# Turning the queries and keys of two attentions before or after they are split into high and low parts

## The chip, the cores and the metric

The kernel runs on one core of a Trainium2 chip. The metric is the device time in microseconds of one execution of the whole program; the time of a version is the median of its runs.

## The reference, cut to what matters

Two layers of a generator's backbone are computed for 512 latent tokens and 256 context tokens of width 1024. Each layer projects the normalised tokens with one matrix `w_in` and feeds four token mixers: a state-space scan, a long convolution, a windowed attention (branch `c` of the kernel) and a dense attention (branch `d`). Their results go through `w_out`, and a squared-ReLU MLP follows. The change lies in the two attentions, in how queries and keys are brought into the form in which the score products take them.

```python
def split_qkv(p):                       # 4 query heads, 2 key and value heads, 64 wide
    q = p[..., :256].reshape(b, n, 4, 64)
    k = p[..., 256:384].reshape(b, n, 2, 64)
    v = p[..., 384:].reshape(b, n, 2, 64)

yw = window_attention(apply_rope(qw, cos, sin), apply_rope(kw, cos, sin), vw, kwc, vwc, attn_sink)
yd = dense_attention(apply_rope(rms_norm(qd, q_norm), cos, sin),
                     apply_rope(rms_norm(kd, k_norm), cos, sin), vd, kdc, vdc)
# the first layer alone also runs both attentions for the context queries
s = jnp.einsum('bqgrd,bkgd->bgrqk', q_blk, k_all) * hd ** -0.5
```

Two query heads (`r`) share one key head: a "group", `kv` in the kernel.

## The kernel before, in words

Tokens lie on partitions, in six tiles of 128: tiles 0 to 3 are latent, 4 and 5 are context. All products use operands in two parts: a high part of 12 bits (type F32R) and the low part that is left. The helper `hi` (L261) writes a high part by a copy on ScalarE, and `lo` (L267, its instruction at L268) subtracts it from the source on VectorE. Weights are split by the same helpers when they are loaded (L354 and L355), so L263 and L268 appear in the rows with many tiles; the tile's name tells them apart.

A layer first runs the two attentions, `d` and then `c` (L1387 to L1392). For each of them:

- `qkv_in` (L1094) projects the tokens. Its results stand in PSUM tiles `pg` (two banks) and are copied by ScalarE to `qk` (L1111, L1113), a tile of 256 query columns and 128 key columns for each token tile.
- `qk_prep` (L1127) normalises (branch `d` alone) and rotates `qk` in place on VectorE, one token tile after the other; L1171 is the last step for a latent tile.
- `qk_split` (L1173) is called once for each of the two groups. For each pair of token tiles it makes tiles `sqk` of 128 x 128: for queries, the high and the low part of each of the two heads, for keys, the high part twice and the low part twice. There are four buffers of `sqk`. Each block of 128 columns is then turned by TensorE (L1204), four blocks to a bank `pm` of PSUM, and the two halves of a bank are copied to the operands `QK` by ScalarE (L1206) and VectorE (L1207). The result is, for each head of queries, a tile whose partitions 0 to 63 hold the high part and 64 to 127 the low part, and for the group's key two tiles, one with the high part in both halves and one with the low part.
- `attend` (L1217) is called for each group, in layer 0 also for the context queries. Scores are two products with these operands (L1247, L1248) into `ps`; then a maximum (L1254), an exponential (L1261) and a normalisation (L1267) give `P`. `P` is turned through `pm` banks (L1284), split to `pt` (`hi` and `lo`) and multiplied with the values into `po` (L1292). At the end of a head the halves of `po` are added (L1295, L1296, both on 64 partitions), which is called the merge below.

Then follow the input projections of the convolution and of the state-space branch (`hyena_in`, `ssd_in`), whose products use the same two `pg` banks. In layer 1 the context tiles have keys but no queries (`need` is false).

The order of the instructions on each engine is not written by hand: a scheduler goes through the program in the order written, with its own estimate of times, and lets work of later calls fill an engine that has nothing to do. So the projection for branch `c` and `hyena_in` run between the steps of branch `d`, and `hyena_in` and `ssd_in` between those of branch `c`. Once ordered, each engine takes its queue in that order: what stands behind a waiting instruction waits too. Banks and buffers are rings: three banks `pm`, two `pg`, one `ps` (two banks wide), one `po`, four `sqk`, eight `QK`.

Of the kernel before, what the change touches and what calls it, by code (L numbers as in the profile page):

```python
# [12 lines left out]
F32 = mybir.dt.float32  # L13
F32R = mybir.dt.float32r
BF16 = mybir.dt.bfloat16
I32 = mybir.dt.int32
AF = mybir.ActivationFunctionType
# [24 lines left out]
# columns of the packed per-partition parameters  # L42
# [3 lines left out]
# columns of the packed row parameters  # L46
# [78 lines left out]
def layout(inp):  # L125
    """The inputs as the program takes them: copies in other orders, nothing computed."""
# [52 lines left out]
def cut(x, c0, n):  # L179
    """token columns c0 .. c0 + n of a (latent, context) pair of tiles"""  # L180
    return x[0][:, c0:c0 + n] if c0 < SEQ else x[1][:, c0 - SEQ:c0 - SEQ + n]


class K:
# [16 lines left out]
    def weave(self, *gens):  # L201
        """emit several streams, each given as (generator, steps per turn)"""
# [26 lines left out]
    def push(self, name, tags, side="left", psum=False):  # L229
        """A phase's pool, tags {tag: (words, dtype, bufs)}; each side is a stack."""  # L230
# [39 lines left out]
    def rsqrt(self, ms, n, w=0):  # L270
        """ms [128, n] -> ms ** -0.5 in a new small tile (Newton from the exponent trick)."""
# [55 lines left out]
    def mlp_order(self):  # L327
        """the units of the two products, an eighth of the hidden features at a time: the second
        product of an eighth comes while the first one of the next is under way."""
# [38 lines left out]
    def tform(self, w, c0, XT, block, m=128):  # L368
        """psum[feat 128, tok] = W chunk^T x; a block of tokens (start, length)."""
# [13 lines left out]
    def nform2(self, ws, X, t, out):  # L383
        """out [tokens of tile t, 512] from four chunks of features."""
# [52 lines left out]
    def mod_section(self, l, s):  # L437
        """silu(c), silu(c_ctx) times columns 1024 s .. of w_mod: two [2, 512] rows."""
# [20 lines left out]
    def mod_sums(self, l, s, hf):  # L459
        """silu(c), silu(c_ctx) times 512 columns of w_mod on the vector engine, 128 partial sums of each."""  # L460
# [18 lines left out]
    def mod_rows(self, acc):  # L479
        """the two sums over the partitions, a row [1, 512] each"""  # L480
# [10 lines left out]
    def mod_cols(self, l, s, idx, gain=None):  # L491
        """shift (or gain * (1 + scale)) with features on partitions: [128, 8, 2]."""
# [65 lines left out]
    def pre_norm(self, xs, xrs):  # L558
        """xr = x * rsqrt(mean(x^2)) for a few tiles at once"""
# [9 lines left out]
    # eight chunks of features by tokens, two parts each: tiles of half the chunks lie together  # L569
# [1062 lines left out]
```

## Time and profile before

| | |
|---|---|
| median of 3 runs | 1932.01 us (1931.42 to 1938.32) |
| span of the profiled execution | 1931.3 us |
| instructions | 27370 |
| TensorE busy, products (PE) and weight loads (PEld) | 1803.7 us and 1480.3 us |
| VectorE (DVE) busy | 1298.2 us |
| ScalarE (ACT) busy | 836.4 us |
| mean granted clock of TensorE | 0.976 |

The profile is of one execution. Products on PE are pipelined, so that the duration of one reaches under the next one, and PE counts as busy in short gaps; on DVE and ACT, too, an instruction can begin a little before the one ahead of it ends. A granted clock of 1.00 is 2.4 GHz and 0.50 is 1.2 GHz. A row of a wait says which instruction waited, which one released it, how long in all, how often, and the longest one.

### The profile page before, as it was taken

The page shows a single profiled execution, that of the slowest core. Times are in us where ns is not written, and L with a number is a line of the kernel's source. Part 1 is how long each engine was busy: PE and PEld are TensorE (multiplying, and loading weights), DVE is VectorE, ACT ScalarE, POOL GpSimd, SP SyncE. Part 2 cuts the span into 40 slices and gives each one's busy share as a digit, 9 for nine tenths or more (in the row PEclk, how much of TensorE's full clock was granted, in tenths as well). Part 3 has the DMA queues.
Part 4 walks back from the last instruction along what each step waited for, and adds up shares of the span by engine and source line. Part 5 has one row for each costly group of instructions (what it writes and reads, how often), then busy time and mean ns, then how long its engine had stood idle before and what let it go on. Part 6 is the DMA issues. An engine that isn't in the chain of part 4 may idle for free.

```text
span 1931.3 us, 27370 instructions
## 1 busy us (share of the span) xinstructions
PE 1803.7 (93%) x10170; PEld 1480.3 (77%) x10170; DVE 1298.2 (67%) x2897; ACT 836.4 (43%) x1804; POOL 91.3 (5%) x176
## 2 busy tenths in 40 slices
PE   6899999979879999999999998899977889999998
PEld 2588888845667888888888888888866688888886
DVE  4877888877656656666666658987878563444446
ACT  3844565536515532322222327556546263232322
POOL 0120001011000000000000000000020000000000
PEclk9999999989989999999999999999989899999999
DMA  7631121278833344333333415122193243233232
GB/s 258 206 118 55 40 72 58 69 255 282 285 99 131 99 131 131 120 112 108 121 120 120 143 46 173 45 56 80 45 297 94 93 143 109 87 99 98 87 101 85
DMA packets 137597, 235.16 MB, mean 122 GB/s; under 512 B 12466, under 2 KB 77395, under 8 KB 137464
## 3 DMA queue, kind: packets, MB, share of 16 engines
q1 hardware_dynamic: 122920, 186.12, 30.2%
q0 software_dynamic: 14544, 47.30, 7.1%
q8 instruction: 80, 1.31, 0.3%
q14 instruction: 53, 0.43, 0.1%
HBM read 206.74 MB, written 26.64 MB: 121 GB/s over the span
## 4 chain that ended last, share of the span: by engine, by line
PE 62%; DVE 7%; ACT 3%; DMA 1%; issue 1%; DVEq 0%; ACTq 0%; SPq 0%
PE pg L296 17%; PE pg L297 16%; PE pg L298 16%; PE py L296 2%; PE py L297 2%; PE py L298 2%; PE po L1292 1%; PE pm L1284 1%; PE ps L1247 1%; PE psd L1050 1%; PE pn L591 0%; PE pm L1204 0%; PE ps L1248 0%; DVE w L268 0%; PE ph L296 0%
## 5 line engine op out<-in xcount | busy, mean ns | idle before, releaser
L263 ACT ACTIVATE w<-r 128x1024 fp32r<-128x1024 f32 (+1 forms) x176 | 186.5, 1061 | 351.2 <-PE pg L298 348.6
L268 DVE TENSOR_TENSOR w<-r,w 128x1024 fp32r<-128x1024 f32 (+1 forms) x176 | 214.3, 1223 | 109.5 <-ACT w L263 108.5
L296 PE MATMUL pg<-xl,w 128*128 128x512 f32 (+1 forms) x704 | 273.0, 391 | 2.5 <-DVE ya L1309 1.4
L298 PE MATMUL pg<-xl,w 128*128 128x512 f32 (+1 forms) x704 | 273.7, 390 | 0.0
L297 PE MATMUL pg<-xl,w 128*128 128x512 f32 (+1 forms) x704 | 272.8, 388 | 0.0
L296 PE MATMUL pg<-w,H 128*128 128x512 f32 x640 | 250.1, 391 | 0.0
L297 PE MATMUL pg<-w,H 128*128 128x512 f32 x640 | 249.3, 390 | 0.0
L298 PE MATMUL pg<-w,H 128*128 128x512 f32 x640 | 249.0, 389 | 0.0
L474 DVE SCALAR_TENSOR_TENSOR x<-r,scT,x 128x512 f32<-128x512 f32 x168 | 119.1, 746 | 70.9 <-DMA r<-in_w_mod_dram 70.9
L296 PEld LDWEIGHTS pg<-xl,w 128*128 128x128 f32 x704 | 132.8, 190 | 30.2 <-issue 2.2
L298 PEld LDWEIGHTS pg<-xl,w 128*128 128x128 f32 x704 | 133.6, 190 | 26.1
L297 PEld LDWEIGHTS pg<-xl,w 128*128 128x128 f32 x704 | 133.8, 190 | 25.6 <-DVE xl L268 0.2
L296 PEld LDWEIGHTS pg<-w,H 128*128 128x128 f32 x640 | 120.1, 188 | 26.9 <-issue 1.8
L1518 ACT ACTIVATE t<-pg 128x512 f32<-128x512 f32 (+1 forms) x100 | 50.4, 506 | 205.7 <-PE pg L298 195.5
L298 PEld LDWEIGHTS pg<-w,H 128*128 128x128 f32 x640 | 120.1, 188 | 24.9
L297 PEld LDWEIGHTS pg<-w,H 128*128 128x128 f32 x640 | 120.1, 188 | 24.7
L1549 DVE TENSOR_TENSOR ya<-pg,ya 128x512 f32<-128x512 f32 x120 | 82.0, 687 | 69.8 <-PE pg L298 69.5
L1520 DVE TENSOR_TENSOR t<-t 128x512 f32<-128x512 f32 (+1 forms) x100 | 58.1, 582 | 89.9 <-ACT H L1519 89.7
L296 PE MATMUL pg<-xc,w 128*128 128x256 f32 (+1 forms) x368 | 103.4, 284 | 1.1 <-ACT xc L263 1.1
L298 PE MATMUL pg<-xc,w 128*128 128x256 f32 (+1 forms) x368 | 104.0, 283 | 0.0
L297 PE MATMUL pg<-xc,w 128*128 128x256 f32 (+1 forms) x368 | 103.9, 283 | 0.0
L296 PE MATMUL pg<-w,xl 128*128 128x256 f32 (+1 forms) x320 | 92.3, 290 | 5.6 <-ACT qk L1111 2.6
(357 smaller groups left out, 3859.2 us busy)
## 6 DMA issues: line engine op xcount, KB each, us to landing
r<-in_mlp_w_dram SPq DMA_DIRECT2D x128, 512.0 KB
r<-in_w_mod_dram SPq DMA_DIRECT2D x80, 512.0 KB
r<-in_w_in_dram SPq DMA_DIRECT2D x40, 512.0 KB
ht<-in_inv_dram POOLq DMA_DIRECT2D x20, 512.0 KB, 5.4
ht<-in_fwd_dram POOLq DMA_DIRECT2D x18, 512.0 KB, 5.3
wm<-in_w_mod_dram SPq DMA_DIRECT2D x16, 512.0 KB
r<-in_w_out_dram SPq DMA_DIRECT2D x16, 512.0 KB
xd<-x POOLq DMA_DIRECT2D x16, 512.0 KB, 3.3
```

What stands on the lines that cost most here:

```text
L263: self.nc.scalar.activation(dst, src, AF.Copy)
L268: self.nc.vector.tensor_tensor(dst, src, h.bitcast(F32), SUB)
L296: mm(out, ah, bh, start=first, stop=False)
L297: mm(out, ah, bl, start=False, stop=False)
L298: mm(out, al, bh, start=False, stop=last)
L474: nc.vector.scalar_tensor_tensor(acc[:, c], raw[:, k], sc, acc[:, c], MUL, ADD)
L1050: nc.tensor.matmul(py[:, 64 * hh:64 * hh + 64], Ms[d][:, hh // 2, hh % 2, :], xdt[:, d, hh, :], start=d == 0, stop=d == 1)
L1247: nc.tensor.matmul(ps[:, o:o + kn], qs, KS[0][:, k0:k0 + kn], start=True, stop=False)
L1284: nc.tensor.transpose(p[:, n:n + 128], P[:, col:col + 128], self.ident)
L1518: nc.scalar.activation(r, p[:, :nn], AF.Relu)
L1520: nc.vector.tensor_tensor(r, r, r, MUL)
L1549: nc.vector.tensor_tensor(dst, p, dst, ADD)
```

## The change

`qk_split` is now called once for both groups. It turns the raw `qk` tiles, 128 columns at a time: the two key heads together, and the two query heads of a group together. The blocks of four latent tiles (or of the two context tiles) go side by side into one `pm` bank. The split is made out of PSUM: ScalarE copies the rows of one head, 64 partitions, to the high part of the operand, and VectorE subtracts that high part from the same rows of PSUM and writes the low part. For a key, both are done twice, once for each half of the partitions. The keys come before the queries. The tiles `sqk` are gone. (The diff also drops comments and docstrings; they are left out here.)

```diff
-    def qk_split(self, l, kv, qk):
+    def qk_split(self, l, qk):
...
-        QS = [self.a("QK") for _ in range(2)]
-        KS = [self.a("QK") for _ in range(2)]
-        for pair in range(3):
-            SQ, SK = [], []
-            for t in (2 * pair, 2 * pair + 1):
-                src = qk[t // 2][:, t % 2]
-                if t < 4 or need:
-                    sq = self.a("sqk", (2, 2, 64))
-                    q_ = src[:, 128 * kv:128 * kv + 128].rearrange("p (h d) -> p h d", d=64)
-                    self.hi(sq[:, :, 0], q_)
-                    self.lo(sq[:, :, 1], q_, sq[:, :, 0])
-                    SQ.append(sq)
-                sk = self.a("sqk", (2, 2, 64))
-                kk = src[:, 256 + 64 * kv:320 + 64 * kv].unsqueeze(1).to_broadcast([128, 2, 64])
-                self.hi(sk[:, 0], kk)
-                self.lo(sk[:, 1], kk, sk[:, 0])
-                SK.append(sk)
-            cs = slice(256 * pair, 256 * pair + 256)
-            jobs = []
-            if SQ:
-                jobs += [([q[:, hh] for q in SQ], QS[hh]) for hh in range(2)]
-            jobs += [([k_[:, hl] for k_ in SK], KS[hl]) for hl in range(2)]
-            for j in range(0, len(jobs), 2):
+        QS = [[self.a("QK") for _ in range(2)] for _ in range(2)]
+        KS = [[self.a("QK") for _ in range(2)] for _ in range(2)]
+        lo, hi = slice(0, 64), slice(64, 128)
+        for t0, cnt in ((0, 4), (4, 2)):
+            n = 128 * cnt
+            cs = slice(128 * t0, 128 * t0 + n)
+            src = [qk[t // 2][:, t % 2] for t in range(t0, t0 + cnt)]
+
+            def turned(c0):
                 p = self.a("pm")
-                for jj in range(2):
-                    for i in range(2):
-                        nc.tensor.transpose(p[:, 256 * jj + 128 * i:256 * jj + 128 * i + 128],
-                                            jobs[j + jj][0][i].bitcast(F32).rearrange("p a d -> p (a d)"), self.ident)
-                nc.scalar.activation(jobs[j][1][:, cs], p[:, 0:256], AF.Copy)
-                nc.vector.tensor_copy(jobs[j + 1][1][:, cs], p[:, 256:512])
-        return QS, KS
+                for i in range(cnt):
+                    nc.tensor.transpose(p[:, 128 * i:128 * i + 128], src[i][:, c0:c0 + 128], self.ident)
+                return p
+
+            p = turned(256)
+            for kv in range(2):
+                r = slice(64 * kv, 64 * kv + 64)
+                H, L = KS[kv]
+                for d in (lo, hi):
+                    nc.scalar.activation(H[d, cs], p[r, :n], AF.Copy)
+                for d in (lo, hi):
+                    nc.vector.tensor_tensor(L[d, cs], p[r, :n], H[r, cs].bitcast(F32), SUB)
+            if t0 == 0 or need:
+                for kv in range(2):
+                    p = turned(128 * kv)
+                    for hh in range(2):
+                        r = slice(64 * hh, 64 * hh + 64)
+                        Q = QS[kv][hh]
+                        nc.scalar.activation(Q[lo, cs], p[r, :n], AF.Copy)
+                        nc.vector.tensor_tensor(Q[hi, cs], p[r, :n], Q[lo, cs].bitcast(F32), SUB)
+        return list(zip(QS, KS))
 
     def attention(self, l, br, qk, V):
-        ops = [self.qk_split(l, kv, qk) for kv in range(2)]
+        ops = self.qk_split(l, qk)
...
         ra = self.push("attR", {"P": (768, F32, 4), "tA": (512, F32, 1), "tP": (384, F32, 2), "yt": (512, F32, 1),
-                                "QK": (768, F32R, 8), "pt": (1024, F32R, 2), "sqk": (256, F32R, 4)}, "right")
+                                "QK": (768, F32R, 8), "pt": (1024, F32R, 2)}, "right")
```

## Rows read from the trace of the kernel before

**Rows 1.** The page, part 1: busy us, share, instructions.

```profile
PE 1803.7 (93%) x10170; PEld 1480.3 (77%) x10170; DVE 1298.2 (67%) x2897; ACT 836.4 (43%) x1804; POOL 91.3 (5%) x176
```

**Rows 2.** The page, part 4: chain that ended last, by engine.

```profile
PE 62%; DVE 7%; ACT 3%; DMA 1%; issue 1%; DVEq 0%; ACTq 0%; SPq 0%
```

**Rows 3.** Stretches of 20 us, layer 0: busy us (instructions), clock, DMA share, GB/s.

```profile
160.00:180.00 20.00, 17.61 (x133) 17.13 (x133) 17.53 (x55) 5.73 (x21) 0.00 (x0) 0.91 0.09 28
180.00:200.00 20.00, 18.68 (x145) 17.05 (x144) 17.34 (x45) 12.93 (x41) 0.00 (x0) 1.00 0.19 54
200.00:220.00 20.00, 19.82 (x154) 18.48 (x153) 18.58 (x48) 11.81 (x30) 0.00 (x0) 1.00 0.00 1
...
280.00:300.00 20.00, 19.76 (x131) 16.80 (x130) 18.68 (x57) 15.49 (x48) 2.16 (x4) 1.00 0.30 93
```

**Rows 4.** The same of layer 1 (PE, PEld, DVE, ACT, POOL as above).

```profile
1220.00:1240.00 20.00, 15.53 (x112) 14.31 (x111) 17.99 (x52) 10.67 (x36) 0.00 (x0) 0.91 0.18 53
...
1320.00:1340.00 20.00, 19.99 (x114) 16.15 (x113) 16.43 (x45) 13.51 (x35) 1.15 (x2) 1.00 0.33 104
```

**Rows 5.** Groups by form, the old split: busy us, mean ns, idle before, releasers.

```profile
L1204 PE MATMUL pm<-ident,sqk 128*128 128x128 f32 x176 | 31.9, 288 | 5.2 <-DVE sqk L268 4.9
L263 ACT ACTIVATE sqk<-qk 128x128 fp32r<-128x128 f32 x88 | 24.3, 306 | 26.8 <-PE pm L1204 14.4 <-DVE qk L1171 10.7 <-ACT qk L1111 0.9
L268 DVE TENSOR_TENSOR sqk<-qk,sqk 128x128 fp32r<-128x128 f32 x88 | 22.3, 284 | 3.6 <-ACT sqk L263 3.4
L1207 DVE CAST QK<-pm 128x256 fp32r<-128x256 f32 x44 | 17.9, 419 | 1.9 <-ACT QK L1206 1.4
L1206 ACT ACTIVATE QK<-pm 128x256 fp32r<-128x256 f32 x44 | 15.9, 376 | 3.7 <-PE pm L1204 3.6
```

**Rows 6.** Timeline of PE in layer 0: start, us, engine, line, count.

```profile
190.33 1.03 PE L1204 MATMUL pm<-ident,sqk 128*128 128x128 f32 x8
191.20 0.27 PE L1284 MATMUL pm<-ident,P 128*128 128x128 f32 x1
```

**Rows 7.** Groups by form: copies and sums out of PSUM.

```profile
L1295 ACT ACTIVATE tA<-po 64x512 f32<-64x512 f32 x16 | 9.5, 593 | 14.3 <-PE po L1292 14.2
L1295 ACT ACTIVATE tA<-po 64x256 f32<-64x256 f32 x8 | 3.0, 380 | 4.1 <-PE po L1292 4.0
L1296 DVE TENSOR_TENSOR yt<-po,tA 64x512 f32<-64x512 f32 x16 | 10.9, 684 | 1.0 <-ACT tA L1295 0.4
L1296 DVE TENSOR_TENSOR yt<-po,tA 64x256 f32<-64x256 f32 x8 | 3.3, 417 | 0.9 <-ACT tA L1295 0.8
L268 DVE TENSOR_TENSOR pt<-pm,pt 128x512 fp32r<-128x512 f32 x80 | 53.0, 687 | 11.6 <-ACT pt L263 10.9
```

**Rows 8.** Timeline of DVE in layer 0, d split and c split.

```profile
189.66 0.89 DVE L268 TENSOR_TENSOR sqk<-qk,sqk 128x128 fp32r<-128x128 f32 x4
...
281.89 0.42 DVE L1296 TENSOR_TENSOR yt<-po,tA 64x256 f32<-64x256 f32 x1
282.33 0.15 DVE L1259 TENSOR_SCALAR s<-s 128x1 f32<-128x1 f32 x1
282.40 0.41 DVE L1207 CAST QK<-pm 128x256 fp32r<-128x256 f32 x1
```

**Rows 9.** Instructions of tile QK, whole program: who waited for it.

```profile
  PEld pm L1204: 0.5, 2
```

**Rows 10.** Waits of PE, whole program: us in total, times, longest.

```profile
PE pm L1204 <- DVE sqk L268: 4.9, 3, 2.4
PE pg L296 <- ACT qk L1111: 2.6, 1, 2.6
```

**Rows 11.** Stretches of 2 us behind the two d splits' stalls.

```profile
176.00:178.00 2.00, 2.00 (x12) 2.00 (x11) 0.57 (x3) 0.30 (x3) 0.00 (x0) 0.50 0.04 8
...
1230.00:1232.00 2.00, 2.00 (x12) 2.00 (x10) 1.61 (x7) 1.76 (x5) 0.00 (x0) 0.50 0.37 77
```

**Rows 12.** Timeline of DVE ahead of layer 0's first transpose.

```profile
171.91 0.55 DVE L1171 TENSOR_TENSOR qk<-qk,tP 128x384 f32<-128x384 f32 x1
...
173.05 0.28 DVE L268 TENSOR_TENSOR sqk<-qk,sqk 128x128 fp32r<-128x128 f32 x1
```

## The prediction

> **What bounds the kernel now.** I read the busy times of the page first: TensorE (PE) is busy for 93% of the span, VectorE (DVE) for 67%, ScalarE (ACT) for 43% [rows 1]. Then the chain of work that ended last: 62% of it lies on PE, and what is not PE is DVE first, 7% [rows 2]. So a time saved on PE is worth most; a time saved on ACT alone is worth nothing in itself. But the change touches only the two attentions of each layer, so the table by stretches of 20 us decides. In layer 0's attention stage PE is busy 19.82 and 19.76 us of 20 in an undisturbed stretch and in the split of branch c, and 17.61 and 18.68 us around the split of branch d [rows 3]; layer 1 looks alike, with 15.53 us around its d split [rows 4]. DVE is close behind in all of them: 17.3 to 18.7 us [rows 3], 16.4 to 18.0 us [rows 4]. Two things are to be seen: PE is the bound, with DVE near enough to take its place, and the two d splits are the two places where PE stands still.
>
> What the split costs now is in the groups by form: 176 transposes, 88 high parts on ACT, 88 low parts on DVE and 44 + 44 copies out of PSUM [rows 5]. The count follows the code: in layer 0 a branch turns 48 tiles into 12 banks, in layer 1, which has no context queries, 40 into 10, and there are two branches each: 2 x (48 + 40) = 176.
>
> **The change part by part.**
>
> *Transposes.* Now a tile of raw queries holds both heads of a group and a tile of raw keys both groups, and no low part is turned. Layer 0: 6 key tiles and 2 x 6 query tiles, 18 for a branch; layer 1: 6 + 2 x 4 = 14. In all 2 x (18 + 14) = 64, so 112 go. Eight in a row took 1.03 us, and a transpose by itself 0.27 us, so each takes (1.03 - 0.27) / 7 = 0.109 us of PE's time [rows 6]: 112 x 0.109 = 12.2 us. The upper bound is the busy time of the group, 31.9 us, by its count: 112/176 x 31.9 = 20.3 us [rows 5]; that counts the latency of each as if nothing ran under it, so I take 12.2. Not all of it shortens the stage: weight loads fill 18.48 of 20 us in one full stretch and 16.80 in another [rows 3], 88% on average, and in the rest PE waits in gaps too short to show. I take 88% of 12.2: **-10.7 us**. This lies on the path because PE has other products at hand in that stage (the next projections), which move up.
>
> *ACT.* Removed: 24.3 + 15.9 = 40.2 us busy [rows 5]. Added: per branch 8 copies of 512 columns and, in layer 0, 8 of 256, in layer 1 only 4; in all 32 and 24, each on 64 partitions. The nearest rows have this shape: 593 ns and 380 ns [rows 7]. 32 x 0.593 + 24 x 0.380 = 28.1 us. ACT is freed of 12 us; the sum counts nothing, because PE covers it.
>
> *DVE.* Removed: 22.3 + 17.9 = 40.2 us [rows 5]. Added: as many subtractions as ACT has copies, PSUM less SBUF on 64 partitions: 684 and 417 ns in the nearest rows [rows 7]; a subtraction over 128 partitions takes 687 ns [rows 7], so half the lanes save nothing. 32 x 0.684 + 24 x 0.417 = 31.9 us. Busy time falls by 8.3 us. Now how far these overlap. Four low parts in a row take 0.89 us at 0.283 each, 0.203 us from start to start [rows 8], so what is removed took 88 x 0.203 + 17.9 = 35.8 us of the engine. A 64-partition sum of the merge starts at 281.89 and takes 0.42, and the next instruction starts at 282.33, behind its end; the one after that starts at 282.40, under the 0.15 us of the one before it [rows 8]. Priced by that row all 56 new ones stand end to end, and DVE is freed of 35.8 - 31.9 = 3.9 us only. The Trainium skill, VectorE: DVE Perf Modes, section Two Vector instructions with no wait between them, says that an instruction whose output starts in another quadrant of partitions than the last one waits until all earlier ones are finished; the new code writes partitions 0 and 64 by turns, so the rule speaks against it, and the row agrees. The forecast's sum doesn't change by it, since it counts nothing for DVE, but it gives the second rival its price.
>
> *PSUM banks.* The bank of a transposed row is read by ACT and DVE in turn. Before, a bank had one copy each: 44 x (0.376 + 0.419) = 35.0 us of holding [rows 5]. After, the keys' latent bank has four and four, 4 x (0.593 + 0.684) = 5.1 us, their context bank 4 x 0.797 = 3.2 us, a query bank two and two, 2.55 or 1.6 us [rows 7]. With 4, 4, 8 and 4 of them: 20.4 + 12.8 + 20.4 + 6.4 = 60.0 us. The extra 25 us, over three banks of the ring, cost PE from 0 to 8.3 us. PE waited 0.5 us in all for a bank to be copied out so far [rows 9], which is next to the lower end: **+1.0 us**.
>
> *The stalls of the d splits.* The first transpose of a split stands in PE's queue until the low part of its tile is there: 4.9 us in three waits [rows 10]; PE waited another 2.6 us for the projection's copy [rows 10] that stood on ACT behind high parts, which waited 10.7 us for the rotation and 14.4 us for a slot of the buffer that the change drops [rows 5]. Behind each of the two stalls the granted clock is 0.50, its lower level of 1.2 GHz, for at least one stretch of 2 us [rows 11], 1.0 us lost each. Upper bound of the gain: 4.9 + 2.6 + 2 x 1.0 = 9.5 us. What will be late next is the rotation itself: the raw transposes wait for it, and in layer 0 the last latent tile's ends at 171.91 + 0.55 = 172.46 us, while the low part that released PE began at 173.05 and ended at 173.33 [rows 12]. That is 0.9 us earlier, and about the same for layer 1: **-1.8 us**. That the row of keys needs four tiles and not two costs nothing here, as the first low part stood behind the fourth tile's rotation anyway [rows 12].
>
> *Waits that are added.* A key row writes the tiles of both groups at once, and the second group's tiles are still read by the scores of the attention before. On ACT stand the projections' and the probabilities' copies behind such a write. I cost it at nothing, because attention d is almost over when the first copy of the c split starts now, at 282.40: its next-to-last head is merged at 281.89 [rows 8], and a head's scores come well before its merge. Without that cover it would be the rest of one context head. No DMA is moved, and neither SP's nor POOL's queue gets another order of its own; the buffer that goes frees space that nobody waits for.
>
> *Sum.* 1931.3 (profiled span) - 10.7 + 1.0 - 1.8 = 1919.8. The median of the runs is 1932.0, 0.7 above the span, so the forecast is **1920.5 us**.
>
> **The rivals.**
>
> *The stalls go as well.* ACT is no longer held by the dropped buffer, copies the projection out in time, and PE runs through the rotation at the full clock: 12.2 + 9.5 = 21.7 us less, 1910.3. For it: the ACT waits of the group [rows 5]. Against: DVE is busy 17.5 us of 20 there [rows 3], and the rotation still must end first.
>
> *DVE takes the place of PE.* The stage then shrinks by what DVE is freed of, 3.9 us: 1928.1. For it: 18.68 of 20 us in the c split, 17.99 in layer 1's d split [rows 3, 4], and the next instruction behind the 64-partition one's end [rows 8]. By the Trainium skill's rule cited above this would be the price of every new subtraction. Against: PE is fuller than DVE in all four stretches of layer 0 [rows 3], and DVE's share of the chain is 7% [rows 2].
>
> *The banks bind: slower.* PE takes its queue in order. If a transpose of the probabilities or the next row stands behind a key bank that is held 5.1 us in place of 0.8, PE stops for 4.3 us and loses another 1.0 us at the lower clock, as behind the stalls of now [rows 11]. In each of the four branches that is 21.2 us, less 10.7: 1942.5. It decides from 10.7 / 4 = 2.7 us a branch on. Against: the 0.5 us of now [rows 9].
>
> *The change does what it says*, but the order of all instructions is worked out anew from the program, and work moves between gaps at no gain: this lies within the second rival's time.
>
> **How the numbers follow.** Forecast 0.50 (own range 1915 to 1925), the stalls go 0.15, DVE binds or no gain 0.27, banks bind 0.08. What a measurement of this kernel can tell from no change is 0.5%, 9.7 us; the bound of faster is 1922.3. Faster: 0.15 and 0.40 of the forecast's 0.50, together 0.55. Within: the other 0.10, 0.27, and 0.02 of the banks: 0.39. Slower: 0.06. The range for 8 in 10 leaves out the banks and the far end of the stalls: 1910 to 1931.
>
> **What would show it.** Right: 64 transposes, PE's busy time down by 12 to 20 us, PE as full in the c splits as now, the wait of the first transpose now put down to the rotation. DVE the bound: its busy share near 20 of 20 us in the stage and PE's below 19. Banks: PE waiting for the new copies out of PSUM by whole microseconds, and more stretches at 0.50. Wrong would make it above all a saving on PE that turns into short gaps, which the 88% only estimates.

## The result, and the profile after

The changed kernel is slower: 1950.83 us in the median (1948.91 to 1956.57), against 1933.24 for the kernel before beside it; the ratio is 1.0092, 95% interval [1.0072, 1.0112]. That is 17.6 us more where the prediction had 11.5 less, and outside its range. The profile is of the slowest of the four executions (1956.57, a span of 1954.8 us), so that against the profiled kernel before (1931.3) it shows 23.5 us of loss and not 17.6.

The page of the changed kernel, part 1 (busy us, share, instructions) and the first line of part 4 (the chain that ended last, by engine):

```profile
PE 1803.2 (92%) x10058; PEld 1484.2 (76%) x10058; DVE 1294.2 (66%) x2821; ACT 832.0 (43%) x1728; POOL 91.9 (5%) x176
...
PE 67%; issue 17%; DVE 8%; DMA 4%; ACT 3%; POOL 2%; SPq 0%; POOLq 0%; DVEq 0%; ACTq 0%
```

Against [rows 1, 2]: 112 matmul records fewer, as the change says, and yet PE is busy as long as before. The mean granted clock is 0.961 instead of 0.976, and at the lower clock a product takes longer: in this trace products of one form (`ph<-hx,ht`) start 0.21 us apart at 420.2 to 423.0 us, where the granted clock is 0.50, and 0.12 us apart at 429.0 to 431.0, where it is 1.00. The chain has a new second entry, "issue", 17%; in the runs below this share does not follow the time (9% in e17, 1% in the slower e18), so nothing is read from it.

The split's groups by form (busy us, mean ns, idle time before, its releasers):

```profile
L1190 PE MATMUL pm<-ident,qk 128*128 128x128 f32 x64 | 11.7, 293 | 8.2 <-DVE qk L1171 6.8 <-DVE QK L1200 1.4
L1209 DVE TENSOR_TENSOR QK<-pm,QK 64x512 fp32r<-64x512 f32 x16 | 11.0, 690 | 1.1 <-ACT QK L1208 0.6
L1200 DVE TENSOR_TENSOR QK<-pm,QK 64x512 fp32r<-64x512 f32 x16 | 11.0, 689 | 7.0 <-ACT QK L1198 6.9
L1198 ACT ACTIVATE QK<-pm 64x512 fp32r<-64x512 f32 x16 | 9.5, 593 | 4.0 <-DVE QK L1200 2.2 <-PE pm L1190 1.5
```

They are what [rows 5] became: 64 transposes, and copies and subtractions at the durations read off [rows 7]. What the change says of its own work it does. So the loss lies elsewhere.

Stretches of 20 us of the changed kernel (us, then busy us and instructions of PE, PEld, DVE, ACT, POOL; granted clock, DMA share, GB/s):

```profile
160.00:180.00 20.00, 17.51 (x140) 16.68 (x140) 18.14 (x36) 9.52 (x19) 0.00 (x0) 1.00 0.09 28
180.00:200.00 20.00, 17.58 (x136) 16.23 (x133) 18.07 (x47) 9.51 (x28) 0.00 (x0) 1.00 0.10 27
...
280.00:300.00 20.00, 19.41 (x128) 17.14 (x128) 17.75 (x35) 13.71 (x28) 2.22 (x4) 1.00 0.12 37
380.00:400.00 20.00, 13.20 (x58) 10.51 (x58) 15.84 (x44) 10.47 (x28) 2.17 (x4) 0.64 0.28 93
400.00:420.00 20.00, 11.60 (x64) 5.41 (x64) 7.24 (x23) 2.70 (x6) 2.15 (x4) 0.50 0.70 222
```

and two of the same stretches of the kernel before:

```profile
380.00:400.00 20.00, 19.30 (x125) 16.36 (x123) 17.36 (x53) 12.44 (x33) 3.24 (x6) 1.00 0.30 102
400.00:420.00 20.00, 10.76 (x59) 4.94 (x63) 14.32 (x28) 6.69 (x14) 2.74 (x5) 0.66 0.92 301
```

Around the two splits the stretches answer to [rows 3] without anything striking. The difference is at 380 to 420 us, where the attention of layer 0 ends. Before, PE is full up to the end (125 instructions) and DVE has 14.32 us of work while the next stage's loads come in. Now 58 instructions are left for PE, its clock is at 0.50, the lower level of 1.2 GHz, and DVE has 7.24 us.

What is missing there lies earlier. Counted in PE's queue, as the traces have it, the products of the next projections that stand ahead of the score tiles of branch c are: before, 19 ahead of the first tile, then 32, 18, 5, 7, and 14, 9, 25, 21, 24, 6 ahead of the last six, some 44 more after that. Now 46, then 38, 47, 10, 13, and 22, 12, 25, 0, 0, 0 ahead of the last six, none after. The program is the same there; its order is not.

The order of issues has changed too. Waits of SP's queue, 370 to 440 us, and its timeline, changed kernel:

```profile
SPq L445 <- PE pg L447: 23.9, 5, 20.6
```

```profile
382.98 23.96 SPq L445 DMA_DIRECT2D r<-in_w_mod_dram  x4
406.99 1.05 SPq L772 DMA_DIRECT2D hz<-us  x2
```

and the timeline of SP's queue before:

```profile
396.36 0.82 SPq L772 DMA_DIRECT2D hz<-us  x2
```

The next stage begins with the loads of `hz`. They were issued 2.0 us ahead of the attention's last merge (398.4 us); now SP stands at a load of the modulation's weights for 20.6 us, and they come 1.3 us behind it (405.7).

By stages, with the exact borders (first sums of branch d's norm to the last merge of branch c, and on to the end of `w_out`; the same for layer 1, and on to its first `w_out` result), before:

```profile
158.97:398.38 239.41, 234.07 (x1578) 206.19 (x1577) 204.27 (x551) 136.31 (x357) 16.41 (x30) 0.99 0.19 60
398.38:618.34 219.96, 185.69 (x1125) 132.99 (x1124) 142.92 (x357) 102.89 (x267) 17.07 (x32) 0.91 0.67 223
1211.63:1405.77 194.14, 185.08 (x1205) 158.68 (x1205) 166.42 (x435) 109.83 (x277) 8.28 (x15) 0.99 0.20 62
1405.77:1523.86 118.09, 89.82 (x494) 71.25 (x493) 88.43 (x189) 54.72 (x150) 11.77 (x22) 0.87 0.54 179
```

and after:

```profile
155.02:405.65 250.63, 235.36 (x1541) 205.56 (x1543) 211.02 (x525) 139.02 (x326) 18.08 (x33) 0.96 0.20 63
405.65:637.86 232.21, 188.98 (x1107) 137.86 (x1096) 134.92 (x344) 98.37 (x258) 15.45 (x29) 0.86 0.61 205
1232.28:1444.55 212.27, 194.16 (x1205) 166.71 (x1204) 177.32 (x416) 115.10 (x254) 11.38 (x20) 0.96 0.24 76
1444.55:1547.56 103.01, 78.57 (x440) 61.94 (x441) 74.68 (x171) 46.78 (x138) 9.04 (x17) 0.87 0.50 165
```

Layer 0 loses 11.2 us in the attention and 12.2 us behind it; layer 1 loses 18.1 in the attention and wins 15.1 behind it, 3.0 us in all. So most of the loss lies in layer 0. (The border at which its attention begins comes 4.0 us earlier in the changed kernel, so that its end comes only 7.3 us later.) The attentions lose time although 60 and 52 transposes have gone from them, and DVE is busy 7 and 11 us longer in them although its split got cheaper: work of the projections has moved in.

### The profile page after: what moved, and what is told of

It is laid out like the page before. It is cut to its first block, busy times and chain, and to the rows that moved or that the text cites. A ratio compares the mean times of both kernels' runs of the same rounds, so it can differ in the third digit from the quotient of the medians.

```text
span 1954.8 us, 26976 instructions
## 1 busy us (share of the span) xinstructions
PE 1803.2 (92%) x10058; PEld 1484.2 (76%) x10058; DVE 1294.2 (66%) x2821; ACT 832.0 (43%) x1728; POOL 91.9 (5%) x176
## 4 chain that ended last, share of the span: by engine, by line
PE 67%; issue 17%; DVE 8%; DMA 4%; ACT 3%; POOL 2%; SPq 0%; POOLq 0%; DVEq 0%; ACTq 0%
PE pg L296 17%; PE pg L297 17%; PE pg L298 17%; PE py L296 2%; PE py L297 2%; PE py L298 2%; PE po L1294 2%; DMA ht<-in_inv_dram 1%; PE pm L1286 1%; PE ps L1249 1%; PE pf L675 1%; PE ps L1250 1%; PE psd L1050 1%; DVE w L268 1%; DMA hf<-spec 0%
```

## The experiments

No kernel below leaves work out. Times are medians, with the ratio to the kernel before on the same chip.

| kernel | split | order | us | ratio, 95% interval |
|---|---|---|---|---|
| changed | new | planned anew | 1950.83 | 1.0092 [1.0072, 1.0112] |
| e1_group | new, by groups | planned anew | 1958.46 | 1.0142 [1.0117, 1.0167] |
| e2_engine | new, copies first | planned anew | 1955.40 | 1.0127 [1.0096, 1.0158] |
| e3_pair | new, 2 tiles a bank | planned anew | 1960.99 | 1.0147 [1.0123, 1.0172] |
| e4_pad | new, 4 KB taken | as changed | 1954.12 | 1.0118 [1.0090, 1.0146] |
| e5_gate | new | 48 products moved back | 1962.07 | 1.0137 [1.0088, 1.0186] |
| e6_double | old, transposes twice | planned anew | 1968.62 | 1.0170 [1.0119, 1.0222] |
| e7_keys | keys new | planned anew | 1949.21 | 1.0074 [1.0051, 1.0097] |
| e8_queries | queries new | planned anew | 1953.94 | 1.0089 [1.0061, 1.0117] |
| e9 | new, modulation moved | attentions as changed | 1966.35 | 1.0164 [1.0147, 1.0181] |
| e10 | old, modulation moved | attentions as before | 1955.96 | 1.0107 [1.0085, 1.0128] |
| e11 | new, modulation earlier | planned anew | 1955.82 | 1.0113 [1.0089, 1.0137] |
| e12_reordered | old, one more buffer | planned anew | 1951.32 | 1.0089 [1.0071, 1.0107] |
| e13 | new | as before | 1943.16 | 1.0047 [1.0029, 1.0065] |
| e14 | old | as changed | 1963.48 | 1.0141 [1.0119, 1.0164] |
| e15 | new | issues alone as before | 1976.97 | 1.0215 [1.0196, 1.0234] |
| e16 | new, by groups | as before | 1948.26 | 1.0071 [1.0050, 1.0092] |
| e17 | queries new | as before | 1944.07 | 1.0066 [1.0044, 1.0088] |
| e18 | new, 2 tiles a bank | as before | 1954.97 | 1.0119 [1.0098, 1.0141] |

### First theory: the products run out before the attention ends

Four kernels change how the new split is laid out. The theory was that the long split of branch c lets the planner pull the projections' products ahead, so that none are left for the attention's end. The rivals were banks of PSUM held too long, and the changed places in SBUF.

```diff
 e1_group: the first group's operands first, the key bank turned once for each group
-            p = turned(256)
-            for kv in range(2):
...
+        for kv in range(2):
+            for t0, cnt, n, cs, src in ranges:
+                key(turned(256, src, cnt), kv, n, cs)
+                query(kv, t0, cnt, n, cs, src)
 e2_engine: all copies of a bank, then all its subtractions
 e3_pair
-        for t0, cnt in ((0, 4), (4, 2)):
+        for t0, cnt in ((0, 2), (2, 2), (4, 2)):
...
-            if t0 == 0 or need:
+            if t0 < 4 or need:
 e4_pad (once a layer; the buffer's tag is back as well)
...
+            for _ in range(4):
+                nc.vector.memset(self.a("sqk")[:, 0:1].bitcast(F32), 0.0)
```

> The new split with the first group's operands brought out first: the key bank is turned once for each group (82 transposes in place of 64, 18 more at 0.11 us = 2 us of PE), the copies and subtractions are the same 56 and 56. Theory (the split's chain up to the first scores has grown, projections were put into it, and none is left beside the last tiles of branch c, so PE stands nearly bare at the lower clock there and behind it): in PE's queue 8 to 20 products now stand ahead of each of the last tiles of branch c where the changed kernel has 0, so the time goes back to 1920 to 1935 us. Rival A (64-partition copies and subtractions are what costs): nothing of them changes, 1948 to 1953 us. Rival B (the freed space moved the buffers of the next stage onto others): unchanged too, 1948 to 1953 us.

> All copies of a bank on ScalarE first, then all its subtractions on VectorE; the same instructions otherwise. In PE's queue layer 0 is as in the changed kernel (0 products ahead of the last three tiles of branch c), layer 1 has 12 to 29 ahead of each of its last tiles again where the changed kernel has 0. Theory: layer 0's loss of some 24 us stays, layer 1's of some 4 us goes: 1944 to 1949 us. Rival A (the turns of the two engines at a bank, and 64-partition work, are the cost): both layers gain alike, 1935 to 1943 us. Rival B (buffers' places): 1948 to 1953 us.

> Two tiles to a bank in place of a row of four, so more and shorter copies and subtractions (80 of each, all of 256 columns, in place of 32 of 512 and 24 of 256: on VectorE 80 x 0.417 = 33.4 us for 31.9). PE's queue has 0 products ahead of the last three tiles of branch c in layer 0, and 12 to 31 in layer 1. Theory: as the engine-by-engine run, 1944 to 1950 us. Rival A (a bank held long is the cost): short holds bring it back in both layers, 1925 to 1938 us. Rival B: 1948 to 1953 us.

> The changed kernel with the 4 KB of the dropped buffer still taken, so that every later buffer lies where it lay before; the order on PE is the changed kernel's. Theory and rival A: no change against the changed kernel, 1948 to 1953 us. Rival B (the places of the next stage's buffers decide which loads wait for the attention's end): back to 1920 to 1935 us.

Measured: 1958.46, 1955.40, 1960.99 and 1954.12 us. The bank rival fell with e3 and the place rival with e4. But the theory fell as it was put, with e1: its queue keeps 11, 20, 15, 8, 14 and 15 products for the last six tiles, as the kernel before does, and it is no faster. In all four the attention of layer 0 takes 250.6 to 252.5 us.

Then the products were held back directly, and the two halves of the change were made alone. In e5 the last quarter of the state-space input takes its banks from the attention's own rings, so it can't start before the last tiles have left them.

```diff
 e5_gate
-                    p = self.tform(w, 128 * c, XT, (o0, nn))
+                    bank = ("ps", "pm")[i % 2] if q == 1 and c == 1 else "pg"
+                    p = self.tform(w, 128 * c, XT, (o0, nn), bank=bank)
 e6_double (kernel before)
-                    for i in range(2):
+                    for i in (0, 0, 1, 1):
 e7_keys, e8_queries: the new split for one of the two, the old one for the other
```

> The changed kernel, with the last products of the state-space input (the last quarter of its x projection, in both layers) put into a score bank and an evacuation bank of the attention instead of the projections' own, so that they can't begin before the attention's last tiles have left these banks. In layer 0 this puts 48 products behind the start of the last score tile, where the kernel before has some 44 and the changed one none. Theory (the fillers run out before the attention ends, and their work on DVE lies inside it): the attention of layer 0 ends 4 to 8 us sooner than in the changed kernel, TensorE's stretch at 0.50 behind it is under 25 us instead of 37.5, and the time is 1938 to 1947. Rival (the new split itself, its chain of ACT and DVE, is what makes the attention longer, wherever the fillers lie): the attention still takes 250 us, the time stays at 1949 to 1956. A third outcome, slower than 1956, would say that the attention's tail wants the products that were taken from it.

> The kernel before, with each of the split's 176 transposes made twice into the same place, so that only TensorE has more to do: 176 x 0.109 us = 19.2 us at full clock. If TensorE's sum sets the time, as the prediction had it for 88% of such work, the time is some 1932 + 17 = 1949. If in the attention something other than TensorE's sum sets the end (the theory now: the chain of the attention over DVE), it is 1930 to 1941.

> One part of the change alone: keys are turned raw, four tiles to a bank, and split on the way out; queries keep the split ahead of the transposes. The order that comes out keeps products for all of the attention's last tiles (23, 27, 19, 14, 13, 15 ahead of the last six in layer 0). Theory (what costs is that no products are left for the end of the attention): 1922 to 1936. Rival (the key bank, held by four copies and four subtractions of 64 partitions one behind the other, is what makes the split slow): 1943 to 1955, about the changed kernel's own.

> The other part alone: queries are turned raw and split on the way out, keys keep the split ahead of the transposes. The order that comes out keeps products for the attention's last tiles too (16, 10, 12, 7, 22, 7 in layer 0). Theory (products left for the end): 1922 to 1938. Rival (the copies and subtractions of 64 partitions cost, in queries as in keys; queries have the smaller number of them to a bank): 1936 to 1946.

Two stretches of e5:

```profile
380.00:400.00 20.00, 15.21 (x56) 12.02 (x57) 9.51 (x42) 7.53 (x23) 1.08 (x2) 0.57 0.12 39
400.00:420.00 20.00, 12.06 (x69) 8.54 (x68) 14.06 (x26) 6.82 (x13) 3.27 (x6) 0.74 0.80 265
```

The work behind the end is back (DVE 14.06 us, 14.32 before), but the attention is only 2.8 us shorter (247.9 us), its tail is still bare, at 0.57, and the stage behind it takes 238.8 us: what was held back is not what stood at the front. e5 is no faster than the changed kernel; its time is in the third outcome (over 1956), though the intervals of the two ratios overlap. In e6 the attention of layer 0 takes 240.9 us, 1.5 more than before with 96 x 0.109 = 10.5 us more for PE, and layer 1's 11.0 more; in layer 0 the projections gave way: ScalarE's last step for them (L912) ends 22.9 us behind the attention instead of 14.0, and the stage behind it is 26.9 us longer. So it answers neither column: 1968.62, twice what the sum of PE gives. e7 and e8 have nearly all of the loss with half of the edit, although products are left at the end. A cost that is about the same for each half and for the whole points to something that the three share, and an order planned anew is such a thing.

### Second theory: transfers bind the stage behind the attention

The DMA share right behind the end of layer 0's attention is 0.92 [the stretch at 400 above], and 32.8 MB moved at 298 GB/s over the 110 us from 398 to 508. Half of that (16.3 MB) are the modulation's weights.

```diff
 e9 (changed kernel), e10 (kernel before)
-ME = (4, 1, 2)
+ME = (4, 0, 3)
 e11 (changed kernel)
+        early = 1 if l == 0 else 0
+        self.do(*self.mod_list(l)[:early])
         self.ssd_in(l, XT)
...
```

> The changed kernel with one of the four modulation sections (eight loads of 512 KB, 4.2 MB) taken from the stage behind layer 0's attention and put among the products of layer 0's MLP, where the transfers' share is 0.38; the order of both attentions stays the same. Theory (in layer 0 the time is the end of the attention plus a stage behind it that is bound by its 33 MB of transfers, 298 GB/s in the kernel before): the stage behind the attention, 118.9 us, shortens by 8 to 15 us (4.2 MB at 273 to 298 GB/s are 14 to 15 us), and the time is 1936 to 1944. Rival (that stage is set by TensorE and its clock, 41 us of it at 0.50): it shortens by no more than the section's 32 small products, 4 us, and the time is 1946 to 1953.

> The same edit on the kernel before, with the order of its attentions unchanged. Theory (transfers bind the stage behind the attention, at a share of 0.91 there): its 110.1 us shorten by 8 to 15 us, and the time is 1918 to 1926. Rival (TensorE): 1929 to 1936.

> The changed kernel with one modulation section of layer 0 (4.2 MB, 32 small products) moved ahead into the attention of layer 0, where the transfers' share is about 0.2; it gets a bank of PSUM of its own there, the attention's evacuation banks are two instead of three. Theory (transfers bind the stage behind the attention): that stage shortens by 8 to 15 us, the attention lengthens by the products (some 4 us) and by what the missing bank costs, 0 to 8: 1936 to 1952. Rival (TensorE binds both stages): the products only move, the bank costs: 1951 to 1960.

Measured: 1966.35, 1955.96 and 1955.82 us. In e9 the stage from the attention's end to the end of `w_out` shortens by 9.3 us (232.2 to 222.9), though up to the state's last sums, the border that the expectation had, by 0.9 only; in e10 it lengthens by 3.1 (220.0 to 223.1), 6.4 up to the nearer border, with 4.2 MB less to move. In the two the MLP takes 17 and 27 us more, and that is most of what they lose. In e11 the stage shortens by 8.8 us (to 223.4), but the attention, with two `pm` banks and the added products, takes 10.9 us more (261.5), and the time is the rival's. So bytes alone don't set that stage, and moving them won nothing; the theory fell. What e9 and e10 do show: with an attention order unchanged, the attention's length repeats, 251.7 against 250.6 us and 238.7 against 239.4, and layer 1's 211.7 against 212.3 and 192.5 against 194.1.

### Third theory: the order

```diff
 e12_reordered (kernel before)
-"sqk": (256, F32R, 4)}, "right")
+"sqk": (256, F32R, 5)}, "right")
```

> The kernel before with a fifth buffer for the split parts, and nothing else: the split, its transposes and its copies are the same, but another order is planned for all engines (15, 29, 13, 16, 11, 2 products ahead of layer 0's last six score tiles instead of 14, 9, 25, 21, 24, 6). If the new split itself lengthens the attention (its 250 us against 239), this one stays near the kernel before: attention of layer 0 at 238 to 243 us, time 1929 to 1937. If any new order of this work loses what the order of the kernel before has, whatever the split: attention 246 to 253 us, time 1942 to 1956.

1951.32 us: one more buffer, nothing in the split or elsewhere rewritten, and the loss is that of the changed kernel. Its stages:

```profile
153.89:396.47 242.58, 235.99 (x1585) 207.62 (x1584) 205.16 (x552) 137.64 (x358) 16.32 (x30) 0.99 0.18 58
396.47:634.03 237.56, 190.18 (x1118) 136.04 (x1117) 142.90 (x357) 102.93 (x267) 17.05 (x32) 0.87 0.62 207
1227.13:1428.45 201.32, 193.15 (x1257) 167.31 (x1256) 174.19 (x451) 114.67 (x287) 10.27 (x18) 0.99 0.21 65
```

It loses in other places: 3.2 us in the attention of layer 0, 17.6 behind it, 7.2 in the attention of layer 1, of which 3.8 come back behind that. And it has 46 products behind the last score tile of layer 0, as the kernel before has 44, and yet its stage behind the attention is the longer one by 17.6 us: where the products lie is not by itself what costs. So my expectation mixed two things: the attention stayed near the kernel before, as the first column has it, and the time is the second column's.

Then the two were separated. In e13 and e14 all instructions outside the split stand in a given order on each engine; only the split's own find their places between them. In the traces these instructions do stand, on all five engines, in the order asked for, and the edges add none: 26976 instructions in e13 as in the changed kernel, 27371 in e14 against 27370 before. e15 gives such an order to the issues on SP and POOL alone.

```diff
 e13: the changed kernel in the order of the kernel before; e14: the other way round
+        own = [x for i, x in enumerate(L) if i not in free and str(x.engine) == "EngineType." + e ...]
+        for a, b in zip(o[:-1], o[1:]):
+            k.tc.add_manual_dep(own[int(b)], own[int(a)].name, info, reason="order")
...
 e15
+    pin(k, ("SP", "Pool"))
```

> The changed kernel, its new split as it is, but every other instruction of all five engines (PE, DVE, ACT, and the issues on SP and POOL) kept in the order that the kernel before has, by edges of order alone, without semaphores; only the split's own instructions find their places between them. If the new order is what costs, and the split itself is worth what the prediction had for it, the time is 1916 to 1928. If the order costs and the split is worth nothing, 1929 to 1936. Rival (the new split itself lengthens the attention, whatever the order): 1942 to 1953.

> The opposite pair: the old split, and every other instruction in the order that the changed kernel has. If the order costs and the split's gain is real: 1951 to 1968 (the changed kernel's time and up to 10 us more for its 112 transposes). Rival (the new split itself costs): 1928 to 1940.

> The changed kernel with the DMA issues alone, those on SP and on POOL, in the order of the kernel before; TensorE, DVE and ACT planned anew, ahead of layer 0's attention tiles as in the changed kernel. If the stage behind the attention is slow because its loads are issued in another order (12 of the 23 us that layer 0 has lost), that stage is back at 220 to 225 us and the time is 1936 to 1943. If the order of the engines' work is what costs, 1946 to 1955.

| | order of before | order of the changed kernel |
|---|---|---|
| old split | 1 (before) | 1.0141 [1.0119, 1.0164] |
| new split | 1.0047 [1.0029, 1.0065] | 1.0092 [1.0072, 1.0112] |

e14's time is in its first column (1951 to 1968). e13's 1943.16 misses the first two and lies in its rival's range (1942 to 1953).

Read down the right column: at the changed kernel's order the new split is worth 1.0092 - 1.0141 = -0.49%, 9.5 us, give or take 5.8 by the two intervals. Read along the upper row: with the old split that order costs 1.41%, 27.3 us. This is one way from the kernel before to the changed one. The other way goes by e13: down the left column the same split costs 0.47%, 9.1 us, and along the lower row the same order costs 0.45%, 8.7 us, give or take 5.2. Each way adds up to the result, so neither share can be named without saying which step comes first.

In e13 and e14 a split stands in an order that was planned for the other one. If this misfit costs as much in the one as in the other, it is (0.47 + 1.41 - 0.92) / 2 = 0.48%; then the order by itself costs 0.93%, 18 us, and the split is worth nothing. e12, in which nothing is crossed, lost 17. That the two misfits are equal is an assumption and not shown. Shown is that the new order costs time with either split, and that what the split is worth changes its sign with the order.

Stages of e14:

```profile
157.79:415.14 257.35, 242.60 (x1601) 212.14 (x1603) 212.50 (x565) 141.64 (x366) 18.01 (x33) 0.96 0.19 61
415.14:642.00 226.86, 183.60 (x1107) 132.59 (x1096) 134.72 (x344) 98.24 (x258) 15.43 (x29) 0.89 0.62 210
1236.02:1451.33 215.31, 200.88 (x1257) 173.29 (x1256) 178.88 (x452) 118.00 (x290) 11.37 (x20) 0.95 0.24 75
```

The old split in this order makes the attentions 6.7 and 3.0 us longer than the changed kernel has them, for 60 and 52 transposes, and the stage behind layer 0's 5.3 us shorter. With the same split as the kernel before they are 17.9 and 21.2 us longer than there: that is the order's doing, the old split's misfit in it included. Behind layer 1's attention 15.1 us come back (118.1 to 103.0 up to the first result of `w_out`), as in the changed kernel: of the 102 products that the kernel before has behind the last score tile there, these two have none left. Stages of e13, its longest wait of PE, and what stands there on PE's timeline:

```profile
158.31:400.98 242.67, 229.03 (x1518) 201.23 (x1517) 203.92 (x511) 134.07 (x317) 16.22 (x30) 0.99 0.18 59
400.98:628.61 227.63, 189.18 (x1125) 136.40 (x1124) 142.93 (x358) 102.93 (x267) 17.11 (x32) 0.89 0.65 215
1221.85:1423.56 201.71, 183.87 (x1153) 158.12 (x1153) 166.00 (x399) 107.54 (x241) 8.22 (x15) 0.96 0.19 59
```

```profile
PE pm L1190 <- DVE QK L1200: 13.9, 5, 4.8
```

```profile
282.76 0.40 PE L296 MATMUL pg<-xl,w 128*128 128x512 f32 x1
286.98 0.83 PE L1190 MATMUL pm<-ident,qk 128*128 128x128 f32 x4 [3.82 <-DVE QK L1200]
```

In the old order PE is busy 5.0 us less in the attention of layer 0 (60 transposes at 0.109 us are 6.5), and idle 8.3 us more (13.6 instead of 5.3): a row of raw transposes stands at a bank that the keys' subtractions still read, with nothing but its own queue behind it. The stage behind it, where neither the order nor the work differs, takes 227.6 us against 220.0, so nothing under 8 us there is read as an effect of an edit. The changed kernel waits for the keys' banks 1.4 us in all. So the planner's new order avoids the wait; that it moved the products for this reason is argued, not shown.

e15 lies outside both columns: with the issues on SP and POOL as before, it is the slowest of all. Its engines were planned anew around these issues and are near the changed kernel's order, not in it (554 of PE's 10058 matmul records stand elsewhere in its queue). Two waits of SP's queue between 370 and 420 us:

```profile
SPq L987 <- DVE P L1271: 21.2, 1, 21.2
SPq L772 <- PE po L1296: 19.3, 1, 19.3
```

Without the order of the engines that it was planned with, this order of issues blocked the queue. Which part of the five orders costs can't be told in this way, and it stays open.

### What the split loses at the old order

```diff
 e16: e1_group's split, e17: e8_queries' split, e18: e3_pair's split, each with
+    pin(k, ("PE", "DVE", "Activation", "SP", "Pool"))
```

> The new split with the first group's operands made first and the key bank turned once for each group (82 transposes, 94 fewer than before), so that every bank of PSUM is held by two copies and two subtractions and not by four of each; all instructions outside the split in the order of the kernel before. Theory (at the old order the changed split loses 7.6 us because TensorE stands at banks that the keys' eight instructions hold, 7.3 us in layer 0 up to the end of branch d): these waits fall under 3 us in layer 0, and the time is 1922 to 1933. Rival (any split other than the one that the order was planned for stalls): 1938 to 1948.

> Queries alone turned raw (136 transposes, 40 fewer than before, each bank held by two copies and two subtractions), keys split as before, all instructions outside the split in the order of the kernel before. Theory (the keys' banks are what stalls): no wait at the keys' banks, 40 x 0.109 = 4.4 us less of TensorE, time 1926 to 1934. Rival (another split stalls at this order): 1937 to 1946.

> The new split with two tiles to a bank instead of a row of four, as many transposes as in the changed kernel (64), twice the copies and subtractions at half their size, all instructions outside the split in the order of the kernel before. Theory (the banks held long are what stalls): each bank is held for about half as long, the waits in layer 0 up to the end of branch d fall from 7.3 to under 4 us, time 1932 to 1940. Rival (the split's whole chain over ACT and DVE sets it, and that gets longer with more instructions): 1943 to 1952.

Measured: 1948.26, 1944.07 and 1954.97 us: the rivals' times in all three, in e16 and e18 at their upper ends or above. Waits of PE in e16, and one in e17:

```profile
PE ps L1256 <- DVE QK L1209: 3.5, 3, 1.6
PE pm L1185 <- DVE QK L1199: 3.1, 4, 2.3
```

```profile
PE pm L1204 <- ACT sqk L263: 8.9, 4, 4.5
```

The waits at the keys' banks did fall, from 13.9 to 3.1 us, but 3.5 us at the scores themselves took their place, and the attention of layer 1 still takes 200.7 us. In e17, where the keys are split as before, PE waits 8.9 us for the high parts of tiles `sqk` on ACT. In e18 the bank waits are 11.1 us. So the banks are one part of what the new split loses in an order made for the old one, and its chain over ACT and DVE probably another, which is argued from these waits and not shown; the rest stays open. No kernel here was faster than the kernel before: each of the nine whose order was planned anew without a hold on it (the changed kernel, e1, e2, e3, e6, e7, e8, e11, e12) lost 0.7 to 1.7%, the most in e6 with its added transposes. Why the order of the kernel before is so much better than all of them is not on record.

## Why the prediction was wrong, point by point

*What bounds.* That PE and DVE are both near full in the attention was right, and for the part which was priced it was enough. It left out the order: where the projections' products lie between the attention's tiles, and the next stage's loads in SP's queue, is planned anew with each edit.

*Transposes, -10.7 us.* Not refuted at the changed kernel's order, where e14 gives 9.5 us, give or take 5.8, and gone at the old one (e13, +9.1). By stages at the new order it is 6.7 us for 60 of them in layer 0 and 3.0 us for 52 in layer 1, 9.8 in all, while the stage behind layer 0's attention, whose length scatters by as much, gives 5.3 back. That 6.7 us are 0.112 us each, so near to the 0.109 of [rows 6], is luck: layer 1 has 0.058. That PE's busy time would fall by 12 to 20 us failed (0.5); the mean granted clock fell with it, from 0.976 to 0.961.

*ACT and DVE.* Sizes right: copies 593 and 591 ns against 593, subtractions 689 and 690 against 684. Two subtractions in a row take 1.40 us of DVE at 283.13 us, end to end, as [rows 8] had it; this trace agrees with the rule cited from the Trainium skill, VectorE: DVE Perf Modes, section Two Vector instructions with no wait between them. DVE's busy time fell by 4.0 us, where the second rival had 3.9; ACT's by 4.4, where 12 were worked out. That their relief counts for nothing was not tested by itself.

```profile
283.13 1.40 DVE L1200 TENSOR_TENSOR QK<-pm,QK 64x512 fp32r<-64x512 f32 x2 [0.81 <-ACT QK L1198]
284.56 0.69 DVE L1209 TENSOR_TENSOR QK<-pm,QK 64x512 fp32r<-64x512 f32 x1
```

*PSUM banks, +1.0.* 1.4 us in the changed kernel, so right there, and 13.9 us in the old order (e13), 3.5 us a branch. The third rival had this mechanism, a transpose standing at a key bank, at 4.3 us a branch and decisive from 2.7 on, with a time of 1942.5; e13 measured 1943.16. So it came near in the order for which the rows were read, though e16 shows that the banks are only part of that loss. In the changed kernel PE hardly stopped there, in its other order.

*Stalls of the d splits, -1.8.* The waits of 4.9 + 2.6 us [rows 10] became 6.8 us, all for the rotation (L1171), which was said to be late next: -0.7.

*The step that failed* is the term for the order, which the sum has at nothing. The prediction says that the order of all instructions is worked out anew, and gives this a lost gain at most, 1928.1 us; for the rest its rows are read as if the order stayed, down to "neither SP's nor POOL's queue gets another order of its own", which was wrong. In its place the runs showed that a new order costs 17 us with no edit of the split (e12), 27.3 us with the old split (e14) and 8.7 us with the new one (the lower row of the table). The term was not mis-sized but missing, with no price on the slow side; that is why the range missed.

Beside it, PE's other products, "which move up", were taken as free, and the place that they left was not looked at: 44 products behind the last score tile of layer 0, and loads that went from 2.0 us ahead of the attention's end to 1.3 us behind it. They did move. That this is what costs is not shown: e5 has 48 products put back and e12 has 46 there, and the stage behind the attention is no shorter in them (238.8 and 237.6 us) than in the changed kernel (232.2). Which part of the new order costs stays open.

## What to carry to other kernels

Where the order of all engines is planned from the whole program, an edit changes the work and the order, and rows price only the first. Here the work was worth -9.5 us in one order and +9.1 in the other, and the order cost 27.3 us with one split and 8.7 with the other. So give the new order a term of its own, sized by an edit that changes no work (one more buffer: +17 us), before a saving of half a per cent is believed; where each newly planned order loses, as here, its price lies on the slow side. To judge the edit, hold everything else in one order, both ways, and read both rows and both columns. And where work "moves up", look at what it covered in the place that it leaves, but test that place before it is called the cause.

## What the runs showed of the hardware

The first 20 us behind layer 0's attention run at the lower clock for the most part in both kernels, at 0.66 and 0.50 [the stretches at 400], while PE is busy for 10.76 and 11.60 us of the 20 and DMA for 0.92 and 0.70 of them. 4.2 MB less to move went with a longer stage there in e10 (223.1 against 220.0 us) and with a shorter one in e9 (222.9 against 232.2).

The attention's length repeats with its order better than that of the stage behind it. Three kernels with the changed kernel's attention order and split took 250.6, 251.8 (e4) and 251.7 us (e9) for layer 0's attention. The stage behind it took 232.2 and 229.1 us in two kernels of one order (the changed one and e4), and, with nothing in it changed, 220.0, 227.6, 225.2, 222.9 and 226.6 us at the order of the kernel before (before, e13, e16, e17, e18). So the 12.2 us that the changed kernel loses there may be scatter in part.
